# Key lengths applied to the token rows of the scores, and group normalisation in token layout, in a hybrid RWKV-7 and convolution decoder step

## The chip, the cores and the metric

The kernel runs on one core of a Trainium2 chip. The core has five engines that work side by side, each in the order of its own instruction list: PE (TensorE, matrix products and transposes into PSUM), DVE (VectorE), ACT (ScalarE), POOL (GpSimd) and SP (SyncE, which here only issues transfers). They wait for each other by semaphores. The metric is the device time of one execution in microseconds (us), lower is better; the median of several executions is compared.

## The reference, cut to what matters

One layer works on 1024 prompt tokens and on 8 short sample sequences of 4 tokens. The input is normalised and projected once; half of the mixing width goes through an RWKV-7 recurrence of 8 heads of 64 channels, the other half through a gated causal convolution; both meet in one output projection. Two places of it matter here: the division of each key by its length, and the two group normalisations over 64 channels of a token.

```python
kk = _heads(kf * k_k)
kk = kk / jnp.maximum(jnp.sqrt(jnp.sum(jnp.square(kk), axis=-1, keepdims=True)), 1e-12)
...
Sk = jnp.einsum('bhvk,bhk->bhv', S, kk_t)
S = S * w_t - Sk[..., None] * (kk_t * a_t)[:, :, None, :] + v_t[..., None] * k_t[:, :, None, :]
y_t = jnp.einsum('bhvk,bhk->bhv', S, r_t)
...
mean = jnp.mean(xg, axis=-1, keepdims=True)
var = jnp.mean(jnp.square(xg - mean), axis=-1, keepdims=True)
y = ((xg - mean) * lax.rsqrt(var + eps)).reshape(xf.shape)
```

The state S sees each normalised key twice in one product (`Sk` and `kk_t * a_t`), so the two inverse lengths of a token always come as their product, one over the squared length.

## The kernel before

**Work.** Channels lie on the 128 partitions, tokens along the free dimension. The input projection is done in blocks of 128 output channels and 256 tokens (`project`, tiles `ps`); its operands are split into a high and a low part (`whi`, `wlo`, `ha`/`hb`), so that each block takes 24 products. Recurrence work comes in units of two 128-channel rows (four heads) by 128 tokens, 16 units and one for the samples. A unit goes through `keys_unit`/`keys_unit2` (decay and keys), `scores_unit` with `masked_scores` (`ap`, `AB`, `Q`), the solution of a triangular system (`blocks_units`, `solve_units`, `solved_units`, `inverse_unit`), `chain_unit` (the recurrence over 64-token chunks, `cb`, `Yp`) and `post_unit` (group normalisation and bonus). The convolution has 16 pieces of 128 channels by 256 tokens (`convolutions`, `cv`), each followed by `post_conv` (group normalisation and swish). `gating` multiplies with the gates, `mixes` reloads the mixed rows, `outputs` does the output projection (`po`), `results` finishes the rows. The sample rows have parts of their own (`chain_sample`, `post_sample`, `outputs_sample`).

**Norms.** All 50 norms (17 of keys, 17 after the recurrence, 16 of the convolution) go through `inverse_norms`: two products with the squares as stationary operand and two columns of ones give sums by token (`n2`, from `arena`), DVE adds the guard, POOL raises to the power -0.5 (`nR`), ACT and POOL split the result into two parts (`nS`), two products with the identity turn it back to channel layout, ACT copies it (`nT`), and one product with `heads4` spreads it over the 64 channels of a head (`bc`), from where DVE multiplies. `group_norm` first takes the mean away by a product with the matrix `bcen` (`yc`).

**Order.** The code is written as some forty strands (generators). A planner (`_Schedule`) runs them at build time: each operation has a modelled cost, each strand a rank, and the operation that can start first is issued next on its engine, a higher rank first. So the order on every engine, SP's transfers included, is fixed before the kernel runs, and it follows from the modelled costs. The strand `filler`, the input projection, has the lowest rank and fills PE where nothing else is ready. All instructions are issued from line 341, so groups are told apart by the tiles they write and read. In the profile's names `n` is the tile `n2`, `arena` is the ring of working tiles, and trailing digits of names are left out.

Of the kernel before, what the change touches and what calls it, by code (L numbers as in the profile page):

```python
# [8 lines left out]
F32 = mybir.dt.float32  # L9
# [395 lines left out]
def hymba_step(ctx, tc, xp, xs, cT, ssT, w_ada, badag, gpost, w_in, wup, par, cst, wkv, cvs, w_out, wdd,  # L405
# [31 lines left out]
    nR = const.tile([128, 19], F32, name="nR")  # L437
    half = nR[:, 18:19]
# [7 lines left out]
    heads4 = const.tile([68, 128], F32R, name="heads4")  # L446
# [8 lines left out]
    for i in range(3):  # L455
        for h in range(2):
            r, a = slice(32 * i, 32 * i + 4), C_ID + 32 * i + h
            V.tensor_tensor(heads4[r, 64 * h:64 * h + 64], cs[r, a:a + 1].to_broadcast([4, 64]),
                            cs[r, a + 2:a + 3].to_broadcast([4, 64]), ALU.add)
# [4 lines left out]
    sl = _Slots({"raw": 2, "ga": 2, "whi": WB, "wlo": WB, "qa": 4, "kb": 2, "unit": 2, "wd": 2, "sh": 2, "wa": 8, "ts": 1, "d2": 2, "dt": 1, "ti": 2}, sched)  # L464
# [502 lines left out]
    def gate(x, p, g, t):  # L967

        keys = [("z", ("c", p), g)] if x == "c" else [("z", p // 2, 2 * g), ("z", p // 2, 2 * g + 1)]
        n = UN + 32 * (x == "c" and g == NU - 1)  # L970
# [81 lines left out]
    def proj_conv(j):  # L1052
# [15 lines left out]
        def ev_c(g, ps, t):  # L1068
            for o, x in parts(t, ps, g):
                S.activation(o, x, AF.Tanh, scale=0.5)  # L1070
                V.scalar_tensor_tensor(o, o, 1.0, x, ALU.add, ALU.mult)
            gate("c", j, g, t)
# [28 lines left out]
    nT = cp1.tile([128, 288], F32R, name="nT")  # L1101
    nRv = nR[:, 0:18].rearrange("p (r i h) -> p r i h", r=3, h=2)
    nS = cp1.tile([128, 3, 3, 4], F32R, name="nS")
    norms = [(r, nRv[:, r], nS[:, r]) for r in range(3)]

    def inverse_norms(nn, n, how, guard):

        while not norms:
            yield BLOCK
        r, R, Rs = x = norms.pop(0)  # L1110
        rows = slice(32 * r, 32 * r + 4)
        whole, rest = divmod(n, 128)
        n2 = yield from bank([128, 512], "n2")
        parts = [(slice(0, whole), 128)] + [(slice(whole, whole + 1), rest)] * (rest > 0)
        for ii, w in parts:
            for i in range(ii.start, ii.stop):
                T.matmul(n2[0:w, 2 * i:2 * i + 2], nn[:, 128 * i:128 * i + w], cs[:, C_ONE:C_ONE + 128:64], start=True, stop=True)
        for ii, w in parts:
            m = ii.stop - ii.start
            nv = n2[0:w, 2 * ii.start:2 * ii.stop].rearrange("p (i h) -> p i h", h=2)  # L1120
            V.tensor_scalar(R[0:w, ii], nv, guard, None, how)
            G.tensor_tensor(R[0:w, ii], R[0:w, ii], half[0:w].unsqueeze(2).to_broadcast([w, m, 2]), ALU.pow)
            S.activation(Rs[0:w, ii, 0:2], R[0:w, ii], AF.Copy)
            G.tensor_tensor(Rs[0:w, ii, 2:4], R[0:w, ii], Rs[0:w, ii, 0:2].bitcast(F32), ALU.subtract)
        for ii, w in parts:
            for i in range(ii.start, ii.stop):
                T.matmul(n2[rows, 128 + 128 * i:128 + 128 * i + w], Rs[0:w, i, :].bitcast(F32), ident[0:w, 0:w],
                         start=True, stop=True)
        S.activation(nT[rows, 0:n], n2[rows, 128:128 + n], AF.Copy)
        drop(n2)  # L1130
        yield
        bc = yield from bank([128, 512], "bc")
        T.matmul(bc[:, 0:n], heads4[rows], nT[rows, 0:n], start=True, stop=True)
        sched.later(lambda: norms.append(x))
        return bc
# [31 lines left out]
    def keys_unit2(p, g):  # L1167
# [5 lines left out]
        bc = yield from inverse_norms(nn, n, ALU.max, 1e-24)  # L1173
# [6 lines left out]
        V.tensor_tensor(kk[:, :n], kr[:, :n], bc[:, :n], ALU.mult)  # L1180
        drop(bc)
# [5 lines left out]
        mark(("keys", p, g), (E, Ei, kk, bt))  # L1187
        yield

    def keys_sample(p, g):  # L1190
# [10 lines left out]
        S.activation(nn[:, :n], kr[:, :n], AF.Square)  # L1201
# [17 lines left out]
    def keys_sample2(p, g):  # L1219
# [5 lines left out]
        bc = yield from inverse_norms(nn, n, ALU.max, 1e-24)  # L1225
# [7 lines left out]
        V.tensor_tensor(kk[:, :n], kr[:, :n], bc[:, :n], ALU.mult)  # L1233
        drop(bc)
# [6 lines left out]
        mark(("keys", p, g), (E, Ei, kk, bt))  # L1241
# [10 lines left out]
    def masked_scores(Q, KB, mask):  # L1252
# [10 lines left out]
        yield  # L1263
        for h in range(2):
# [4 lines left out]
            V.tensor_tensor(AB[H[h]].rearrange("p c a s -> p c (a s)")[:, :, a:128], aps[h][H[h], :, a:128],  # L1269
                            cs[H[h], mask + a:mask + 128].unsqueeze(1).to_broadcast([64, NCH, 128 - a]), ALU.mult)  # L1270
        for h in range(2):
# [7 lines left out]
    def scores_unit(p, g):  # L1279
# [4 lines left out]
        E, Ei, kk, bt = done["keys", p, g]  # L1284
# [12 lines left out]
        ec = w2.tile([128, 4], F32, tag="ec", name="ec", bufs=4)  # L1297
        V.tensor_copy(ec, tok65(E)[:, :, 64])
        give(E, Ei, kk, bt)
        for i, cc in both(p):  # L1300
            V.scalar_tensor_tensor(km[:, cc], km[:, cc], hp[:, 33 + i:34 + i], R[:, cc], ALU.mult, ALU.mult)
        AB = yield from masked_scores(Q, KB, C_MP)
        for c in range(NCH):
            S.activation(KB[:, c], KB[:, c], AF.Copy, scale=ec[:, c:c + 1])
        mark(("scores", p, g), dict(Q=Q, AB=AB, KB=KB, ec=ec))
# [16 lines left out]
    def scores_sample(p, g):  # L1322
# [3 lines left out]
        E, Ei, kk, bt = done["keys", p, g]  # L1326
# [14 lines left out]
        es = w1.tile([128, 4 * NB], F32, tag="es", name="es")  # L1341
# [736 lines left out]
```

## Time and profile before

| | |
|---|---|
| median of 3 runs | 866.58 us (866.39 to 872.11) |
| the profiled execution, its own time | 874.14 us |
| its span, first to last instruction | 872.4 us |
| mean granted TensorE clock in it | 0.975 |

The profiled execution is 7.6 us slower than the median. In the lists of the trace a row "x4" is four records; a product of full 32-bit operands leaves two records, one of the split parts or a transpose leaves one. The duration of a record reaches over the next ones, because products are pipelined: what a group costs PE is better read as the distance from its start to the start of the next group.

### The profile page before, as it was taken

To read this page: it belongs to the slowest core of one execution; us is meant where nothing else is said; L and a number is where in the kernel's file an instruction comes from. 1 tells how busy PE (TensorE), PEld (TensorE's weight loads), DVE (VectorE), ACT (ScalarE), POOL (GpSimd) and SP (SyncE) were. 2 spreads that over 40 slices of the span, in tenths; PEclk is the share of its full clock that TensorE was granted. 3 is DMA by queue.
4 is the path that set the end of the run, shared out by engine and by line. 5 is a ranking of instruction groups with operands and counts; after the bars stand their busy time and mean duration, and the time that the engine had idled before them with its cause. 6 is when DMAs were issued, how large, how long until landed. Compare 5 with 4: busy or idle time off the path is not lost.

```text
span 872.4 us, 23611 instructions
## 1 busy us (share of the span) xinstructions
PE 815.5 (93%) x9050; PEld 666.9 (76%) x9050; DVE 417.3 (48%) x1012; ACT 462.8 (53%) x1276; POOL 402.5 (46%) x759
## 2 busy tenths in 40 slices
PE   4868999999999999999999999999999999599995
PEld 2647888897889778888789878788987997475763
DVE  4556443562455554562662655574766363113122
ACT  4447577556676366672584567576655564211201
POOL 3237456463447216234325343644753765534332
PEclk9999899999999999999999999999999999698998
DMA  9987889788546753438735736435693676765432
GB/s 322 314 271 242 278 295 323 226 268 251 165 129 207 184 152 114 137 110 247 208 105 171 235 100 201 135 123 184 210 296 110 194 225 184 210 224 193 156 121 85
DMA packets 147729, 172.38 MB, mean 198 GB/s; under 512 B 23296, under 2 KB 105600, under 8 KB 147616
## 3 DMA queue, kind: packets, MB, share of 16 engines
q1 hardware_dynamic: 147328, 170.28, 63.0%
q8 instruction: 71, 1.16, 0.6%
q10 hardware_dynamic: 288, 0.59, 0.2%
q14 instruction: 42, 0.34, 0.1%
HBM read 112.68 MB, written 58.13 MB: 196 GB/s over the span
## 4 chain that ended last, share of the span: by engine, by line
PE 69%; DMA 14%; DVE 5%; ACT 4%; POOL 3%; issue 3%; SPq 1%; POOLq 0%; DVEq 0%; ACTq 0%
PE ps L341 30%; PE po L341 8%; PE cv L341 6%; PE n L341 4%; PE cb L341 4%; DMA wa<-w_ada 3%; PE ap L341 3%; PE Yp L341 2%; DMA xt<-xp 2%; PE yc L341 2%; PE p L341 2%; SPq L341 1%; PE bc L341 1%; DMA wd<-wdd 1%; ACT arena L341 1%
## 5 line engine op out<-in xcount | busy, mean ns | idle before, releaser
L341 PE MATMUL ps<-hb,whi 128*128 128x258 f32 (+3 forms) x928 | 199.0, 301 | 0.0
L341 PE MATMUL ps<-ha,whi 128*128 128x256 f32 (+2 forms) x864 | 180.9, 301 | 4.3 <-ACT ha L341 3.2
L341 PEld LDWEIGHTS ps<-hb,whi 128*128 128x128 f32 x928 | 149.6, 189 | 6.3 <-issue 2.7
L341 PEld LDWEIGHTS ps<-ha,whi 128*128 128x128 f32 x864 | 138.5, 191 | 14.8 <-issue 4.0
L341 PE MATMUL ps<-hb,wlo 128*128 128x258 f32 (+3 forms) x464 | 140.1, 302 | 0.0
L341 PE MATMUL ps<-ha,wlo 128*128 128x256 f32 (+2 forms) x432 | 130.9, 303 | 2.4 <-POOL wlo L341 2.4
L341 POOL TENSOR_TENSOR wlo<-raw,whi 128x512 fp32r<-128x512 f32 x58 | 78.4, 1352 | 66.1 <-ACT whi L341 50.2
L341 POOL TENSOR_TENSOR nR<-nR 128x4 f32<-128x4 f32 (+2 forms) x56 | 55.8, 998 | 77.5 <-DVE nR L341 77.2
L341 PEld LDWEIGHTS ps<-hb,wlo 128*128 128x128 f32 x464 | 87.6, 189 | 3.4 <-issue 1.2
L341 PEld LDWEIGHTS ps<-ha,wlo 128*128 128x128 f32 x432 | 82.4, 191 | 7.6 <-POOL wlo L341 3.0
L341 PE MATMUL cv<-SH,wd 128*32 128x256 f32 x1024 | 61.7, 389 | 4.0 <-DMA kept<-wlo 2.2
L341 ACT ACTIVATE arena<-ps,hp 128x256 f32<-128x256 f32 (+3 forms) x72 | 32.2, 455 | 51.7 <-PE ps L341 45.5
L341 ACT ACTIVATE X<-AB,cs 32x64 f32<-32x64 f32 x136 | 54.7, 403 | 2.1
L341 PEld LDWEIGHTS cv<-SH,wd 128*32 128x32 f32 x1024 | 35.1, 112 | 23.5 <-issue 2.7
L341 DVE SCALAR_TENSOR_TENSOR arena<-arena 128x256 f32<-128x256 f32 (+1 forms) x64 | 33.6, 527 | 34.3 <-DMA arena<-prj_a 13.1
L341 DVE TENSOR_TENSOR arena<-arena,bc 128x256 f32<-128x256 f32 (+2 forms) x50 | 20.6, 414 | 58.7 <-PE bc L341 56.2
L341 POOL TENSOR_TENSOR Ti<-Ti,tm 128x15 f32<-128x15 f32 (+4 forms) x135 | 41.1, 304 | 8.8
L341 ACT ACTIVATE whi<-raw 128x512 fp32r<-128x512 f32 x58 | 36.3, 626 | 15.6 <-DMA raw<-w_in 11.2
L341 POOL TENSOR_TENSOR tm<-D,Ti 128x15 f32<-128x15 f32 (+4 forms) x135 | 39.5, 293 | 10.2 <-DVE D L341 1.2
L341 ACT ACTIVATE arena<-arena 128x256 f32<-128x256 f32 (+3 forms) x100 | 41.1, 415 | 2.8 <-DVE ec L341 0.6
L341 DVE SCALAR_TENSOR_TENSOR arena<-ps,pr,arena 128x256 f32<-128x256 f32 (+4 forms) x40 | 17.5, 441 | 50.4 <-ACT arena L341 50.0
L341 POOL TENSOR_TENSOR arena<-arena,mx 128x256 f32<-128x256 f32 (+2 forms) x32 | 25.1, 785 | 35.3 <-ACT mx L341 31.8
(204 smaller groups left out, 1652.4 us busy)
## 6 DMA issues: line engine op xcount, KB each, us to landing
whi<-kept SPq DMA_DIRECT2D x52, 256.0 KB, 3.0
wlo<-kept SPq DMA_DIRECT2D x52, 256.0 KB, 3.8
raw<-w_in SPq DMA_DIRECT2D x50, 256.0 KB, 3.8
kept<-whi SPq DMA_DIRECT2D x44, 256.0 KB, 3.4
kept<-wlo SPq DMA_DIRECT2D x44, 256.0 KB, 3.2
wa<-w_ada SPq DMA_DIRECT2D x32, 256.0 KB, 5.4
SH<-gld SPq DMA_DIRECT2D x48, 142.0 KB, 4.0
xt<-xp SPq DMA_DIRECT2D x8, 512.0 KB, 5.4
```

The costliest lines, as they stand in the source:

```text
L341: emit = lambda: f(*a, **k)
```

## The change

Four things change.

1. `inverse_norms` is gone, with `nR`, `nS`, `nT` and `heads4`. For the keys, `square_sums` takes its place: eight products of a 64x64 block of squares with one column of ones, whose result lies with tokens on the partitions; DVE applies the guard (`n2s`).
2. The keys stay undivided (the product of `kr` with `bc` is left out). `scores_unit` takes the reciprocal of the squared lengths (`inv`, in the tile `er`), and `masked_scores` multiplies the token rows of the score block with it; this was a copy on ACT and is now a product on DVE. In `chain_unit` the two copies that negate the solved rows now multiply with `inv` (two ACT instructions and one DVE instruction where there were one and one), and the sign moves to the copy `Wt`.
3. `group_norm` transposes the tile to token layout (`tp`), takes the sum, the difference and the squares there (two reductions and two more operations on DVE, one square on ACT), raises and multiplies on POOL, and transposes back (`yc`). It returns the PSUM tile, and the caller's next operation reads it.
4. The 32 sample tokens of the convolution, which were appended to the last piece of each of four channel rows (288 columns), get a strand of their own, `post_conv_sample`, for all four rows; `gating` then always works on 256 columns.

```diff
+    def square_sums(nn):
+        n2 = yield from bank([128, NCH], "n2")
+        for u in range(NCH):
+            for h in range(2):
+                T.matmul(n2[H[h], u:u + 1], nn[H[h], 64 * u:64 * u + 64], cs[H[h], C_ONE + 64 * h:C_ONE + 64 * h + 1],
+                         start=True, stop=True)
...
+        V.tensor_scalar(t, n2, 1e-24, None, ALU.max)
...
-        bc = yield from inverse_norms(nn, n, ALU.max, 1e-24)
+        n2 = yield from square_sums(nn)
...
-        V.tensor_tensor(kk[:, :n], kr[:, :n], bc[:, :n], ALU.mult)
-        drop(bc)
...
+        V.reciprocal(inv, n2)
...
             if a:
-                S.activation(AB[H[h], :, 0, :], aps[h][H[h], :, 0:64], AF.Copy)
+                V.tensor_tensor(AB[H[h], :, 0, :], aps[h][H[h], :, 0:64], iv(h), ALU.mult)
...
-            S.activation(Wt, cb[:, 0], AF.Copy)
+            S.activation(Wt, cb[:, 0], AF.Copy, scale=-1.0)
...
-            S.activation(mv[H[0], :, c, 0, :], cb[H[0], 1], AF.Copy, scale=-1.0)
-            V.tensor_scalar(mv[H[1], :, c, 1, :], cb[H[1], 1], -1.0, None, ALU.mult)
+            for i, u in slots:
+                S.activation(MV[H[0], u, 0, :], cb[H[0], 1, i], AF.Copy, scale=inv[H[0], i, c:c + 1])
+            V.tensor_tensor(mv[H[1], :, c, 1, :], cb[H[1], 1], inv[H[1], :, c].unsqueeze(2).to_broadcast([64, 2, 64]), ALU.mult)
...
     def group_norm(src, n, guard):
-        yc = yield from bank([128, 512], "yc")
-        T.matmul(yc[:, :n], bcen, src, start=True, stop=True)
...
-        bc = yield from inverse_norms(q, n, ALU.add, guard)
-        V.tensor_tensor(q[:, :n], src, bc[:, :n], ALU.mult)
...
+        tp = yield from bank([128, 2, 128], "tp")
+        for i, w in tiles:
+            T.transpose(tp[0:w, i, :], src[:, 128 * i:128 * i + w], ident)
...
+            V.tensor_reduce(a, by_group(tp, ii, w), mybir.AxisListType.X, ALU.add)
+            V.tensor_scalar(a, a, 1.0 / 64, None, ALU.mult)
+            V.tensor_tensor(by_group(qv, ii, w), by_group(tp, ii, w), spread(a), ALU.subtract)
+            S.activation(sq[0:w, ii], qv[0:w, ii], AF.Square, scale=0.125)
+            V.tensor_reduce(b, by_group(sq, ii, w), mybir.AxisListType.X, ALU.add)
+            G.tensor_scalar(b, b, 1.0, guard, ALU.mult, ALU.add)
+            G.tensor_tensor(b, b, half[0:w].unsqueeze(2).to_broadcast([w, m, 2]), ALU.pow)
+            G.tensor_tensor(by_group(qv, ii, w), by_group(qv, ii, w), spread(b), ALU.mult)
...
+        for i, w in tiles:
+            T.transpose(yc[:, 128 * i:128 * i + w], qv[0:w, i, :], ident[0:w, 0:w])
...
+    def post_conv_sample():
+        yield from wait(*(("acc", j) for j in range(4)), *(("out", "c" + str(j), NU - 1) for j in range(4)))
...
+        Z.dma_start(out=mixd[4:8, :, SEQ:NT].rearrange("k p t -> p k t"), in_=side(z))
```

The planner makes a new order out of this. A program that lists each engine's instructions gives these pieces; a row is an instruction or several alike in a row (x2), `out<-in`, partitions x elements.

PE in the second half of the input projection, before, where the norms of three tiles meet recurrence work:

```order
L341 MATMUL bc<-nT,heads_126 128x256
L341 MATMUL za<-tw,wu 128x128 x2
L341 MATMUL cb<-Wt,TT 64x64 x4
L341 MATMUL n_7458<-cs,arena 128x2 x2
L341 MATMUL vt<-cs,arena 128x128 x2
L341 MATMUL yc<-arena,cs 128x256
L341 MATMUL ps<-hb,whi 128x256
L341 MATMUL n_7481<-cs,arena 128x2
L341 MATMUL cb<-MV,KTt 64x64 x4
L341 MATMUL Yp<-AB,MV 64x64 x2
L341 MATMUL n_7481<-cs,arena 128x2
```

The same engine and about the same place now:

```order
L341 MATMUL cv<-SH,wd 32x256 x32
L341 MATMUL cb<-MV,KTt 64x64 x4
L341 MATMUL Yp<-AB,MV 64x64 x4
L341 MATMUL n_7471<-cs,arena 64x1 x8
L341 MATMUL yc<-cs,arena 128x128 x2
L341 MATMUL tp<-cs,arena 128x128
L341 MATMUL kt<-cs,KB 128x128 x4
L341 MATMUL tp<-cs,arena 128x128 x3
```

In the place of the products `n`, `bc` and the wide `yc` stand single-column products and transposes.

PE at the samples' group normalisation in the output projection, before:

```order
L341 MATMUL yc<-arena,cs 128x160
L341 MATMUL po<-ha,mh 128x512 x2
L341 MATMUL po<-ha,ml 128x512 x2
L341 MATMUL n_10932<-cs,arena 128x2
L341 MATMUL n_10932<-cs,arena 32x2
L341 MATMUL n_10932<-cs,nS 4x128
L341 MATMUL n_10932<-cs,nS 4x32
L341 MATMUL bc<-nT,heads_126 128x160
L341 MATMUL po<-ha,mh 128x512 x2
```

And now:

```order
L341 MATMUL Yp<-Q,MV 64x64 x8
L341 MATMUL tp<-cs,arena 128x128
L341 MATMUL po<-ha,mh 128x512 x2
L341 MATMUL po<-ha,ml 128x512 x2
L341 MATMUL po<-ha,mh 128x512 x4
L341 MATMUL po<-ha,ml 128x512 x2
L341 MATMUL po<-ha,mh 128x512 x4
L341 MATMUL po<-ha,ml 128x512 x2
L341 MATMUL yc<-cs,arena 128x128
```

Four output products stood between `yc` and the first `n`, and none between the two kinds of `n`; now sixteen stand between the transpose there and the one back.

POOL at the same place (`hb<-wo` splits the output weights, `ml` the mixed rows, `nR` is the power), before:

```order
L341 TENSOR_TENSOR hb<-wo,hb 128x512 x3
L341 TENSOR_TENSOR nR<-nR 128x2
L341 TENSOR_TENSOR nR<-nR 32x2
L341 TENSOR_TENSOR nS<-nR,nS 128x2
L341 TENSOR_TENSOR ml<-raw,mh 128x512
L341 TENSOR_TENSOR hb<-wo,hb 128x512 x2
L341 TENSOR_TENSOR nS<-nR,nS 32x2
```

And now, with the statistics in `st`:

```order
L341 TENSOR_TENSOR ml<-raw,mh 128x512
L341 TENSOR_SCALAR st_205<-st_205 128x2
L341 TENSOR_TENSOR st_205<-st_205,half 128x2
L341 TENSOR_TENSOR hb<-wo,hb 128x512 x3
L341 TENSOR_TENSOR arena<-arena,st_205 128x128
```

The last POOL step of the norm stood behind two weight splits, and stands behind three.

More of the change, by code (lines that the diff above doesn't have):

```diff
@@ L1099, in tok65 @@
         return t[:, 0:260].rearrange("p (c s) -> p c s", s=65)
[L1101 to L1127, printed above, removed]
@@ L1128, in inverse_norms @@
+    norms = [cp1.tile([128, 2, 2, 2], F32, name=f"st{r}") for r in range(4)]
+    def square_sums(nn):
[3 more added lines that the diff above has]
+                T.matmul(n2[H[h], u:u + 1], nn[H[h], 64 * u:64 * u + 64], cs[H[h], C_ONE + 64 * h:C_ONE + 64 * h + 1],
                          start=True, stop=True)
-        S.activation(nT[rows, 0:n], n2[rows, 128:128 + n], AF.Copy)
+        yield from sl.need("n2")
+        t = w2.tile([128, NCH], F32, tag="n2", name="n2s", bufs=4)
+        V.tensor_scalar(t, n2, 1e-24, None, ALU.max)
@@ L1130, in inverse_norms @@
         drop(n2)
[L1131 to L1135, printed above, removed]
+        return t
     def keys_unit(p, g):
@@ L1186, in keys_unit2 @@
         give(nn)
-        mark(("keys", p, g), (E, Ei, kk, bt))
+        mark(("keys", p, g), (E, Ei, kk, bt, n2))
         yield
@@ L1345, in scores_sample @@
         V.tensor_tensor(pairwise(km), pairwise(km), per_pair(-33, 40), ALU.mult)
-        AB = yield from masked_scores(Q, KB, C_MS)
+        AB = yield from masked_scores(Q, KB, C_MS, inv)
         for a in range(2):
@@ L1664, in group_norm @@
     def group_norm(src, n, guard):
[L1666 to L1677 removed]
+        while not norms:
+            yield BLOCK
+        st = norms.pop(0)
+        whole, rest = divmod(n, 128)
+        parts = [(slice(0, whole), 128)] * (whole > 0) + [(slice(whole, whole + 1), rest)] * (rest > 0)
+        tiles = [(i, w) for ii, w in parts for i in range(ii.start, ii.stop)]
+        tp = yield from bank([128, 2, 128], "tp")
+        for i, w in tiles:
+            T.transpose(tp[0:w, i, :], src[:, 128 * i:128 * i + w], ident)
+        q = yield from take("nt", "q")
+        by_group = lambda t, ii, w: t[0:w, ii].rearrange("p i (h v) -> p i h v", h=2)
+        qv = q[:, 0:256].rearrange("p (i c) -> p i c", i=2)
+        sq = src[:, 0:256].rearrange("p (i c) -> p i c", i=2)
+        for ii, w in parts:
+            m = ii.stop - ii.start
+            spread = lambda a: a.unsqueeze(3).to_broadcast([w, m, 2, 64])
+            a, b = st[0:w, ii, :, 0], st[0:w, ii, :, 1]
+            V.tensor_reduce(a, by_group(tp, ii, w), mybir.AxisListType.X, ALU.add)
[6 more added lines that the diff above has]
+            G.tensor_tensor(by_group(qv, ii, w), by_group(qv, ii, w), spread(b), ALU.mult)
+        drop(tp)
+        yield
+        yc = yield from bank([128, 256], "yc")
+        for i, w in tiles:
+            T.transpose(yc[:, 128 * i:128 * i + w], qv[0:w, i, :], ident[0:w, 0:w])
+        sched.later(lambda: norms.append(st))
+        return q, yc
     def post_unit(p, g):
@@ L1842, in sample_block, with swish @@
         yield
+    def swish(z, q, yc, gains):
+        for cc, a, b in gains:
+            S.activation(z[:, cc], yc[:, cc], AF.Identity, scale=a, bias=b)
+        n = gains[-1][0].stop
+        drop(yc)
+        S.activation(q[:, 0:n], z[:, 0:n], AF.Tanh)
+        V.scalar_tensor_tensor(z[:, 0:n], q[:, 0:n], 1.0, z[:, 0:n], ALU.add, ALU.mult)
     def post_conv(first, step):
@@ L1859, in post_conv @@
             yield
+    def post_conv_sample():
+        yield from wait(*(("acc", j) for j in range(4)), *(("out", "c" + str(j), NU - 1) for j in range(4)))
+        z = yield from take("nt", "z")
+        side = lambda t: t[:, 0:128].rearrange("p (k t) -> p k t", k=4)
+        Z.dma_start(out=side(z), in_=accd.rearrange("k p t -> p k t"))
+        t = yield from take("gt", "gate")
+        for j in range(4):
+            Z.dma_start(out=t[:, 32 * j:32 * j + 32], in_=prj["c" + str(j)][:, SEQ:NT])
+        q, yc = yield from group_norm(z, 128, 1e-5)
+        swish(z, q, yc, [(slice(32 * j, 32 * j + 32), hp[:, 45 + j:46 + j], hp[:, 49 + j:50 + j]) for j in range(4)])
+        V.scalar_tensor_tensor(z[:, 0:128], z[:, 0:128], 0.5, t[:, 0:128], ALU.mult, ALU.mult)
+        Z.dma_start(out=mixd[4:8, :, SEQ:NT].rearrange("k p t -> p k t"), in_=side(z))
+        give(z, q, t)
+        mark(("mix", "cs"))
+        yield
     oq = []
@@ L1919, in outputs_sample @@
     def outputs_sample():
-        yield from wait("gates", ("y", 0, NE - 1), ("y", 1, NE - 1), ("mix", SMP), *(("mix", ("c", k), NU - 1) for k in range(4)))
+        yield from wait("gates", ("y", 0, NE - 1), ("y", 1, NE - 1), ("mix", SMP), ("mix", "cs"))
         m = yield from take("nt", "m")
```

94 lines of the change are left out of this document (45 added, 49 removed).

## The prediction

> **What bounds the kernel now.** I read the page first: the busy shares and the chain of work that ended last.
>
> ```profile
> span 872.4 us, 23611 instructions
> ...
> PE 815.5 (93%) x9050; PEld 666.9 (76%) x9050; DVE 417.3 (48%) x1012; ACT 462.8 (53%) x1276; POOL 402.5 (46%) x759
> ...
> PE 69%; DMA 14%; DVE 5%; ACT 4%; POOL 3%; issue 3%; SPq 1%; POOLq 0%; DVEq 0%; ACTq 0%
> ```
>
> PE is busy for all but 57 us and makes up most of the chain; the other engines are about half used. Next I cut the span into stretches (busy time of each engine, granted clock, share of the DMA engines) and asked what PE waited for.
>
> ```profile
> 100.00:200.00 100.00, 98.52 (x1067) 82.61 (x1069) 52.77 (x121) 64.17 (x173) 53.92 (x102) 0.97 0.88 286
> 600.00:700.00 100.00, 97.37 (x1111) 84.36 (x1110) 57.04 (x147) 57.15 (x163) 55.23 (x117) 0.98 0.65 201
> ...
> PE ada L341 <- DMA wa<-w_ada: 14.5, 8, 9.0
> PE n L341 <- POOL nS L341: 8.9, 2, 5.4
> ...
> POOL nR L341 <- DVE nR L341: 77.2, 32, 7.4
> ```
>
> From 100 us on PE hardly stops. Its largest wait lies ahead of that, the next is one place in the tail, and POOL waits much longer for PE's results than PE for POOL's. So a change counts here by the PE time it takes away or adds, if the new order keeps PE fed. How many norms there are, and where:
>
> ```profile
> L341 PE MATMUL n<-cs,arena x208: 165/251/273, 94.1 to 746.6; 128*128 128x2 f32 x98, 128*32 128x2 f32 x6
> L341 PE MATMUL n<-cs,nS x208: 184/273/418, 98.7 to 756.3; 128*4 128x128 f32 x98, 32*4 32x32 f32 x6
> L341 PE MATMUL bc<-nT,heads x50: 336/380/498, 100.9 to 756.9; 4*128 4x256 f32 x44, 4*128 4x288 f32 x4, 4*128 4x160 f32 x2
> L341 PE MATMUL yc<-arena,cs x66: 298/379/510, 149.7 to 745.1; 128*128 128x256 f32 x56, 128*128 128x288 f32 x8, 128*128 128x160 f32 x2
> ```
>
> Fifty `bc` are fifty norms; 66 records of `yc` are 33 group normalisations, so 17 norms are of keys. All lie between 94 and 757 us, where PE is the bound.
>
> **PE's part of the sum.** Two pieces of PE's timeline hold nearly every operation that goes, and the nearest rows to those that come (start, length, group).
>
> ```profile
> 319.72 0.38 PE L341 MATMUL bc<-nT,heads 4*128 4x256 f32 x1
> 320.02 0.66 PE L341 MATMUL kt<-cs,KB 128*128 128x128 f32 x4
> 320.52 0.60 PE L341 MATMUL bo<-arena,cs 128*128 128x256 f32 x2
> 320.95 0.59 PE L341 MATMUL yc<-arena,cs 128*128 128x256 f32 x2
> 321.48 0.45 PE L341 MATMUL cb<-Wt,TT 64*64 64x64 f32 x8
> 321.86 0.61 PE L341 MATMUL n<-cs,arena 128*128 128x2 f32 x4
> 322.32 0.41 PE L341 MATMUL vt<-cs,arena 128*128 128x128 f32 x2
> 322.49 0.38 PE L341 MATMUL ps<-hb,whi 128*128 128x296 f32 x1
> ...
> 733.79 2.04 PE L341 MATMUL sp<-Q,M 64*64 64x16 f32 x64
> 735.76 0.60 PE L341 MATMUL n<-cs,nS 128*4 128x128 f32 x4
> 736.29 0.51 PE L341 MATMUL po<-ha,mh 128*128 128x512 f32 x1
> ```
>
> From start to next start: `n` from `arena` 0.46, `n` from `nS` 0.53, `bc` 0.30, together 1.29 us for a norm; fifty are 64.5 us. `yc` took 0.53 here, and `bo`, of the same form, 0.43; I take 0.43, for 33 that is 14.2 us. Removed: 78.7 us. The ends are 64.5 + 33 x 0.24 = 72.4 (0.24 is half of the mean of `bo` and `yc`, one of the two records) and 64.5 + 17.5 = 82.
>
> Added for the keys: 17 times eight products, 16 records with 64x64 weights. The row nearest in columns is `sp`: 64 records in 1.97 us, so 16 in 0.49; the row nearest in place is `cb`: 8 in 0.38, so 0.76. Near the first, with a little for the changed shape, I take 0.55: 9.4 us (8.3 to 12.9).
>
> Added for the group normalisations: 67 transposes there and 67 back (two each, and one more of 32 tokens for the samples of each way). Four `kt` took 0.50, two `vt` 0.17; I take a pair at 0.25, the longer: 67 pairs, 16.8 us (11.4 to 16.8).
>
> Net: 78.7 - 9.4 - 16.8 = 52.5 us off PE, between 72.4 - 12.9 - 16.8 = 42.7 and 82 - 8.3 - 11.4 = 62.3.
>
> On transposes the Trainium skill speaks against the change: "TensorE: Matmul & The Clock Gate", Part 4, gives about 275 ns for one of 128x128 in a kernel's context and says that they do not count as activity for the clock. By that 134 would be an estimated 36.9 us and the net gain 32.4 us. The `kt` and `vt` rows, 0.125 and 0.085 us each, are for back-to-back ones in this kernel and disagree, and the granted clock was 1.00 from 150 to 200 us, with `kt` and `vt` in it (the rows of the stretches below), so the sum goes by them.
>
> **The other engines.** Durations of the removed operations and of the nearest ones to the new (busy time, mean ns of one, idle time before; the last row, of PE, is for a rival below):
>
> ```profile
> L341 POOL TENSOR_TENSOR nR<-nR 128x4 f32<-128x4 f32 x48 | 50.1, 1044 | 77.5 <-DVE nR L341 77.2
> L341 POOL TENSOR_TENSOR TT<-T,cs 128x256 f32<-128x256 f32 x17 | 11.5, 678 | 30.2 <-DVE T L341 30.2
> L341 DVE TENSOR_TENSOR arena<-arena,bc 128x256 f32<-128x256 f32 x44 | 18.2, 416 | 51.2 <-PE bc L341 50.8
> L341 DVE TENSOR_REDUCE accs<-arena 128x8 f32<-128x248 f32 x16 | 6.5, 406 | 6.0 <-POOL arena L341 5.9
> L341 ACT ACTIVATE AB<-ap 64x256 f32<-64x256 f32 x32 | 12.0, 376 | 9.7 <-PE ap L341 7.5 <-DVE Q L341 1.7
> L341 ACT ACTIVATE nT<-n 4x256 fp32r<-4x256 f32 x44 | 16.4, 373 | 22.9 <-PE n L341 22.1
> L341 PE MATMUL tp<-cs,xt 128*128 128x128 f32 x64 | 11.0, 317 | 2.6 <-DVE xt L341 2.6
> ```
>
> DVE: a group normalisation gains two reductions of about 0.41 (the new ones read 256 elements, the row 248) and loses nothing large, since the difference with 0.42 takes the place of the product with `bc`: 33 x 0.82 = 27 us. A unit of keys loses the product with `bc` and gains two products of 0.42 in `masked_scores`: 17 x 0.42 = 7 us. DVE goes from 417 to about 451 us, 55% of the new time. ACT loses `nT` fifty times and `AB` 32 times, 31 us. POOL loses 17 powers of 1.04 and gains 33 products of about 0.68: 5 us more. All of it lies beside PE: none of the three comes near PE's load, and what hides it is the projection (`ps`), which in the new order still stands between recurrence, transposes and convolution up to the first output products. If that cover were gone, a group normalisation would expose two reductions, a difference, a square, a power and a product in a row, 3.0 us by these rows with the square left aside, against a longer row of PE, DVE, POOL and ACT steps before. `chain_unit` gets a second ACT step in a row in each of its 32 steps; behind it wait only that unit's next products. The extra transfers (four loads and four stores of 32 columns for the samples' gate, fewer for `accd`) are six more on SP's queue by the lists of both programs. I count all this as nothing.
>
> **The tail.** The one long wait is in the samples' normalisation:
>
> ```profile
> 746.20 0.53 PE L341 MATMUL n<-cs,arena 128*128 128x2 f32 x4
> 752.15 0.59 PE L341 MATMUL n<-cs,nS 128*4 128x128 f32 x2 [5.42 <-POOL nS L341]
> 756.23 0.27 PE L341 MATMUL n<-cs,nS 32*4 32x32 f32 x2 [3.49 <-POOL nS L341]
> ...
> 753.33 2.50 POOL L341 TENSOR_TENSOR hb<-wo,hb 128x512 fp32r<-128x512 f32 x2
> 755.77 0.41 POOL L341 TENSOR_TENSOR nS<-nR,nS 32x2 fp32r<-32x2 f32 x1
> ...
> 815.82 21.38 PE po L341 x91
> ```
>
> POOL's steps stand behind splits of output weights that arrive late. In the new order sixteen output products (16 x 21.38 / 91 = 3.8 us, by the last row, from the chain) come in between, but the last POOL step stands behind three splits instead of two. I leave this wait as it is; its 9 us are the most that could be gained here.
>
> **What is taken off.** The transfers keep their volume while the projection gets shorter. The stretches where they are densest, with the records of `n` in each and the DMA share:
>
> ```profile
> 100.00:150.00 50.00, 2.31 (x16) 1.66 (x16) 0.33 (x2) 0.92 (x3) 0.93 0.93 309
> 150.00:200.00 50.00, 4.51 (x32) 3.17 (x32) 0.64 (x4) 1.49 (x4) 1.00 0.83 262
> 600.00:650.00 50.00, 3.77 (x28) 2.54 (x28) 0.54 (x4) 1.42 (x4) 1.00 0.75 228
> 700.00:750.00 50.00, 3.30 (x24) 2.31 (x24) 0.59 (x5) 0.77 (x2) 1.00 0.67 199
> ```
>
> The first two hold 48 of 416 records, 12% of the gain, 6 us; I take half of it as lost, 3 us, and as much again for new short waits of PE at the transposes back, which join POOL's queue. So 52.5 - 6 = 46.5 us. Against the profiled execution's own 874.1 us that is 827.6; against the median, 7.6 us lower, 820 us.
>
> **Rivals.**
> - *The gain holds* (70%): 820 us, from 803 (the upper net, nothing lost) to 838.
> - *Transfers hold it back* (12%): all four stretches of the last rows keep their length, 100 of 416 records or 24%, 13 us, and PE's waits for loads grow by as much again. Then 26 of the 52.5 us are lost: 866.6 - 52.5 + 26 = 840 us. For it speaks the share of 0.93, against it that PE there is still 98.5% busy.
> - *Transposes are dear* (6%): each advances PE by the whole mean length of such a record where the input is transposed, 0.317 us (row `tp` above), instead of 0.125: 134 x 0.317 = 42.5 us instead of 16.8, so 820 + 26 = 846 us. Against it: `kt` and `vt`, which stand in the same stretch of the program as the new ones. The Trainium skill's rule above ("TensorE: Matmul & The Clock Gate", Part 4) would come out near this, at an estimated 840.
> - *Waits take the place of the work* (7%): PE stops at each transpose back. The break-even is 52.5 / 33 = 1.6 us of waiting per normalisation, at which the time stays within 1% of 866.6. Against it: the same kind of join in the kernel before, fifty times, cost 8.9 us in all.
> - *Slower* (5%): POOL's queue becomes late as a whole, with its new last step (0.68 us) behind splits of 1.3 us. It decides from 1.85 us per normalisation (61 us); at half of the 5.42 us of the tail's wait, 2.7 us, the time is 866.6 - 52.5 + 89 = 903 us. For it speaks that such a wait exists; against it POOL's idle 77 us ahead of `nR`.
>
> That the operations stay is no rival: the lists of the new program hold none of the removed products.
>
> **How the numbers follow.** About 1% is what a measurement of this kernel can tell from no change. The first three cases are faster by more than that: 0.88; the fourth is the same, 0.07; the fifth slower, 0.05. The range from 802 to 844 takes in the first case and the second, 82%, and leaves out the other three.
>
> **What would show it.** In the new profile PE's busy time should be some 50 us lower, 94 to 97% of the part from 100 us to the first `po`; the first `po` should start some 45 us earlier; `tp` and `yc` pairs should advance by 0.25 us and the eight `n` by 0.55. DVE should show about 450 us, ACT about 430, POOL about 405. Wrong would be: PE waits for POOL's or DVE's normalisation steps of more than 10 us outside the tail, a lower granted clock between 100 and 700 us, or waits for `whi`, `wd` and `SH` loads that grow to tens of microseconds.

## The result and the profile after

| | kernel before | changed kernel |
|---|---|---|
| median, same chip | 869.35 us (866.39 to 878.21, 4 runs) | 833.25 us (829.40 to 835.91, 4 runs) |
| ratio of the two | | 0.9565, 95% interval 0.9481 to 0.9649 |
| the profiled execution, its own time | 874.14 us | 832.94 us |

The changed kernel is faster by 4.4%, some 36 us by the medians and 41.2 us between the two profiled spans (872.4 and 831.2 us). The profiled execution of before is 4.8 us above its median, that of the changed kernel at its median. The page of the changed kernel, its busy times and its chain of work:

```profile
span 831.2 us, 23357 instructions
...
PE 758.8 (91%) x8924; PEld 634.7 (76%) x8924; DVE 454.2 (55%) x1111; ACT 423.9 (51%) x1143; POOL 401.6 (48%) x753
...
PE 57%; DMA 20%; ACT 6%; DVE 6%; SPq 4%; issue 3%; POOL 2%; POOLq 0%; DVEq 0%; ACTq 0%
```

PE does 56.7 us less, DVE 37 more, ACT 39 less, POOL the same. PE's share of the chain fell from 69% to 57%: PE is still the bound, but it is fed less closely. The same is seen when the span is cut at the first output product (stretch, its length, PE's busy time and records, granted clock, share of the DMA engines, GB/s). First the kernel before:

```profile
100.00:723.00 623.00, 614.42 (x7696) 0.99 0.63 191
723.00:872.40 149.40, 126.12 (x721) 0.91 0.52 166
```

And the changed kernel:

```profile
100.00:690.40 590.40, 567.69 (x7695) 0.99 0.67 203
690.40:831.20 140.80, 116.59 (x586) 0.92 0.53 172
```

From 100 us to the first output product PE's busy time fell by 46.7 us, the stretch only by 32.6: PE's idle time there grew from 8.6 to 22.7 us. The tail lost 9.5 us of PE time and 8.6 us of length. What ended PE's waits between 100 us and the first output product, longest sums first (us in all, times, longest); the kernel before, and in the second fence the changed kernel:

```profile
PE cv L341 <- DMA kept<-wlo: 2.2, 1, 2.2
PE cv L341 <- DMA wd<-wdd: 1.7, 2, 1.1
PE yc L341 <- ACT arena L341: 1.0, 1, 1.0
```

```profile
PE cb L341 <- ACT MV L341: 3.0, 4, 0.8
PE cv L341 <- DMA wd<-wdd: 2.8, 2, 1.5
PE cv L341 <- DMA SH<-gld: 2.5, 3, 1.1
PE sp L341 <- DMA M<-wkv: 1.6, 1, 1.6
PE ps L341 <- POOL wlo L341: 1.5, 3, 0.6
PE kt L341 <- ACT KB L341: 1.4, 1, 1.4
PE cb L341 <- issue: 1.3, 1, 1.3
PE cv L341 <- DMA whi<-kept: 1.3, 1, 1.3
```

No single wait explains the 14 us: there are many of 1 to 3 us, more than a third of their sum for loads. The longest sum is new: products of the recurrence (`cb`) that wait for ACT's scaled rows `MV`, a step that the change made longer. PE's waits for the normalisation steps of DVE and POOL do not appear, outside one place in the tail. The new operations in the table by line and form (busy time, mean ns of one, idle time of the engine before them):

```profile
L341 PE MATMUL tp<-cs,arena 128*128 128x128 f32 x66 | 13.9, 284 | 1.0 <-ACT arena L341 0.8 <-ACT TT L341 0.2
L341 PE MATMUL n<-cs,arena 64*64 64x1 f32 x272 | 11.1, 194 | 0.1
L341 DVE TENSOR_REDUCE st<-tp 128x4 f32<-128x256 f32 x32 | 13.4, 421 | 12.2 <-PE tp L341 12.0
L341 POOL TENSOR_TENSOR arena<-arena,st 128x256 f32<-128x256 f32 x32 | 20.3, 636 | 1.7
L341 ACT ACTIVATE MV<-cb,er 64x64 f32<-64x64 f32 x64 | 18.6, 308 | 27.9 <-PE cb L341 13.0 <-DVE MV L341 10.4 <-POOL tm L341 4.0
L341 DVE TENSOR_TENSOR MV<-cb,er 64x128 f32<-64x128 f32 x32 | 9.4, 295 | 30.8 <-ACT MV L341 24.0 <-POOL Ti L341 3.3 <-POOL arena L341 1.2
```

The last two rows are the recurrence's step. Each names the other as what ended its waits (10.4 and 24.0 us), and in the trace ACT's and DVE's parts of a step never overlap; in 21 of the 32 steps the DVE instruction stands between the two of ACT. From the start of the first instruction of a step to the end of the last, the median step takes 1.05 us. In the kernel before, with these two rows (shortest, median and longest in ns; 32 of the 33 are of the chain), it takes 0.67 us:

```profile
L341 ACT ACTIVATE MV<-cb x33: 258/270/377, 163.6 to 741.9; 64x128 f32<-64x128 f32 x32, 64x256 f32<-64x256 f32 x1
L341 DVE TENSOR_SCALAR MV<-cb x33: 294/294/429, 164.0 to 742.4; 64x128 f32<-64x128 f32 x32, 64x256 f32<-64x256 f32 x1
```

Over 32 steps, at 0.38 us each, the chain is some 12 us longer, of which PE waits for as much as it has no other work for.

The tail keeps its long wait. PE and POOL there (start, length, group, idle time before it):

```profile
704.06 0.62 PE L341 MATMUL po<-ha,ml 128*128 128x512 f32 x2
704.52 1.09 PE L341 MATMUL po<-ha,mh 128*128 128x512 f32 x4
705.45 0.63 PE L341 MATMUL po<-ha,ml 128*128 128x512 f32 x2
714.38 0.47 PE L341 MATMUL yc<-cs,arena 128*128 128x128 f32 x1 [8.29 <-POOL arena L341]
...
717.27 1.22 PE L341 MATMUL po<-ha,mh 128*128 128x512 f32 x2 [1.14 <-ACT arena L341]
718.29 0.63 PE L341 MATMUL po<-ha,ml 128*128 128x512 f32 x1
718.71 1.91 PE L341 MATMUL po<-ha,mh 128*128 128x512 f32 x4
```

```profile
709.57 0.71 POOL L341 TENSOR_TENSOR st<-st,half 128x2 f32<-128x2 f32 x1
710.25 3.72 POOL L341 TENSOR_TENSOR hb<-wo,hb 128x512 fp32r<-128x512 f32 x3
713.91 0.41 POOL L341 TENSOR_TENSOR arena<-arena,st 128x128 f32<-128x128 f32 x1
```

The samples' last normalisation step (713.91) stands behind three weight splits of 3.72 us, which PE waits for. But the chain that ended last does not run through POOL here. It runs through the load of the mixed rows (start, length, what):

```profile
712.27 3.13 DMA raw<-mixd
...
716.05 1.18 ACT arena L341 x4
717.22 0.04 issue
717.27 0.80 PE po L341
```

ACT splits these rows first (from 715.51) and reads `yc` only then (716.05), and PE's second wait, of 1.14 us, ends with that. By these rows a shorter queue on POOL alone would move three records of output products ahead, and not the rest.

After the second wait three records of output products take 1.44 us (717.27 to 718.71), 0.48 each, where two took 0.46 together ahead of the long wait (704.06 to 704.52); the granted clock says why (stretches of 5 us of the changed kernel):

```profile
700.00:705.00 5.00, 5.00 (x37) 1.00 0.87 261
705.00:710.00 5.00, 1.08 (x5) 0.94 0.59 194
710.00:715.00 5.00, 0.62 (x2) 0.50 0.54 158
715.00:720.00 5.00, 3.86 (x10) 0.50 0.50 138
720.00:725.00 5.00, 5.00 (x17) 0.69 0.71 203
```

The clock is at half some 3 us after PE's last product (which ended at 706.1; 0.94 is full clock up to about 709.4), and the 0.69 puts its return at about 723, some 9 us after PE's work began again, with the second wait in between. PE worked between 7 and 8 us at half rate, so by this estimate the wait of 8.3 us costs three to four more. The Trainium skill ("TensorE: Matmul & The Clock Gate", Part 1) states such a gate, half rate after an idle window of about 3.4 us and full rate after a busy window of that length; the rows agree on the first and show a longer way back, which holds the second wait. The kernel before pays about the same at its own wait (clock 0.50 from 750 to 760 us, 0.66 from 760 to 765), so this is no difference between the two.

### The profile page after: what moved, and what is told of

Same layout as the page of the kernel before. It is cut to its first block, busy times and chain, and to the rows that moved or that the text cites. A ratio compares the mean times of both kernels' runs of the same rounds, so it can differ in the third digit from the quotient of the medians.

```text
span 831.2 us, 23357 instructions
## 1 busy us (share of the span) xinstructions
PE 758.8 (91%) x8924; PEld 634.7 (76%) x8924; DVE 454.2 (55%) x1111; ACT 423.9 (51%) x1143; POOL 401.6 (48%) x753
## 4 chain that ended last, share of the span: by engine, by line
PE 57%; DMA 20%; ACT 6%; DVE 6%; SPq 4%; issue 3%; POOL 2%; POOLq 0%; DVEq 0%; ACTq 0%
PE ps L341 25%; PE po L341 10%; PE cv L341 5%; SPq L341 4%; PE cb L341 4%; ACT arena L341 3%; DMA SH<-gld 3%; PE Yp L341 2%; DMA gld<-arena 2%; PE ap L341 2%; DMA kept<-whi 2%; DMA arena<-prj_a 2%; DVE arena L341 2%; DMA xt<-xp 1%; DMA arena<-zd 1%
## 5 line engine op out<-in xcount | busy, mean ns | idle before, releaser
L341 PE MATMUL ps<-ha,whi 128*128 128x256 f32 (+2 forms) x864 | 178.6, 300 | 3.8 <-ACT ha L341 2.9
L341 PE MATMUL cv<-SH,wd 128*32 128x256 f32 x1024 | 58.6, 380 | 7.9 <-DMA wd<-wdd 2.8
L341 ACT ACTIVATE arena<-arena 128x256 f32<-128x256 f32 (+5 forms) x103 | 41.7, 409 | 16.2 <-DVE arena L341 11.4
L341 PE MATMUL po<-ha,mh 128*128 128x512 f32 x128 | 40.2, 433 | 2.5 <-DVE M L341 1.4
L341 ACT ACTIVATE mh<-raw 128x512 fp32r<-128x512 f32 x16 | 10.1, 631 | 57.5 <-DMA raw<-mixd 47.0
L341 DVE TENSOR_TENSOR Q<-arena 64x256 f32<-64x256 f32 (+1 forms) x68 | 36.6, 540 | 0.6
```

The lines of the kernel that those rows point to most:

```text
L341: emit = lambda: f(*a, **k)
```

## The experiments

The first theory was that the PE work taken off is the whole gain, and that what is missing was lost to waits which the change itself made: the longer step of the recurrence and the samples' wait in the tail. The rival was that the planner's new order decides: any edit changes the modelled costs, the planner places hundreds of instructions otherwise, and the time moves with that. Runs e1 to e4 ran on one chip (kernel before 872.97 us, 7 runs), e5 to e8 on a second (869.24 us, 11 runs), e9 to e12 on a third (869.60 us, 23 runs). Each ratio is to the kernel before on the same chip, so runs of different chips are better compared by their ratios.

**e1, the keys' part alone.** From the kernel before: `square_sums`, `inv`, the scores and `chain_unit` of the change; `group_norm` as it was.

```diff
-        bc = yield from inverse_norms(nn, n, ALU.max, 1e-24)
+        n2 = yield from square_sums(nn)
```

> The kernel before with the key part of the change alone (squared lengths applied to token rows, no transposes). Theory 1 (the gain is PE work, the loss is many small waits spread over the program): PE busy falls by 11 to 13 us against before (17 norms at 1.29 less 0.55), PE's idle time between 100 and 700 us rises by 3 to 5 us, the time falls by 8 to 10 us, to about 858. Rival (the second ACT step in the recurrence carries most of the 15 us of new waits): PE idle rises by 8 us or more here, waits of cb for ACT MV of 3 us and more, and the time falls by 4 us or less.

Measured: 859.42 us, ratio 0.9858 (0.9808 to 0.9908). PE's busy time is 800.7 us, 14.8 less than before. From 100 to 700 us PE is idle for 12.8 us instead of 8.6, as theory 1 had it, and its waits of `cb` for ACT's `MV` sum to 1.0 us. The time fell by more than theory 1's 8 to 10 us, and the gain stands in the tail: the first output product starts at 724.2 us instead of 723.0, and the tail is 132.9 us long instead of 149.4.

**e2, the group normalisation alone.** From the changed kernel: the keys divided and normed as before, and the recurrence's step as before.

```diff
-        n2 = yield from square_sums(nn)
+        bc = yield from inverse_norms(nn, n, ALU.max, 1e-24)
```

> The kernel before with the group normalisation part alone (transposes; keys still divided through the old norms). Theory 1: PE busy falls by 40 to 46 us, PE idle rises by 8 to 12 us, the time falls by some 32 us, to about 836. Rival (the waits belong to the key part): PE idle stays within 4 us of before's 38 and the time falls by 40 us or more, to under 829.

Measured: 844.33 us, ratio 0.9677 (0.9644 to 0.9711). PE's busy time is 779.6 us, 35.9 less than before. The two parts save 13.6 and 28.6 us; together that is 42 us, where the whole change saves 36 to 37 (e5). The keys' part gave about what the prediction's terms make of it (17 x 1.29 - 9.4 = 12.5 us), though where it gave it owes something to the order; the normalisation's part gave less (33 x 1.29 + 14.2 - 16.8 = 40 us). Ahead of the first output product, which starts at 664.9 us here, PE is idle for 7.1 us, less than before. So the 14 us of new idle time there are not the sum of the two parts: the keys' part alone shows 4 of them, the normalisation alone none. In the tail of e2 PE waits 5.2 us for finished output rows of DVE and 4.2 us for POOL at a transpose back.

**e3, both halves of the solved rows scaled on DVE.** The changed kernel without the two ACT instructions of the recurrence's step.

```diff
-            for i, u in slots:
-                S.activation(MV[H[0], u, 0, :], cb[H[0], 1, i], AF.Copy, scale=inv[H[0], i, c:c + 1])
-            V.tensor_tensor(mv[H[1], :, c, 1, :], cb[H[1], 1], inv[H[1], :, c].unsqueeze(2).to_broadcast([64, 2, 64]), ALU.mult)
+            for h in range(2):
+                V.tensor_tensor(mv[H[h], :, c, h, :], cb[H[h], 1], inv[H[h], :, c].unsqueeze(2).to_broadcast([64, 2, 64]), ALU.mult)
```

> The changed kernel, but both halves of the solved rows are multiplied on DVE, so the recurrence has one DVE step more and no ACT step there. If the second ACT step costs what the waits of cb for ACT MV show (3.0 us in four places), those waits go and the time falls by about 3 us against the changed kernel, to 830. If PE's small waits only move to the next late operand: the waits for ACT MV go, waits for DVE come, the time stays within 1% of 833.

Measured: 822.48 us, ratio 0.9415 (0.9357 to 0.9472), 1.5% below the changed kernel's and more than either expectation. The step is now two DVE instructions, 0.61 us, and PE's idle time between 100 us and the first output product is halved:

```profile
L341 DVE TENSOR_TENSOR MV<-cb,er 64x128 f32<-64x128 f32 x64 | 18.5, 289 | 27.6 <-PE cb L341 22.0 <-POOL arena L341 1.9 <-POOL st L341 1.8
...
100.00:657.60 557.60, 545.89 (x7399) 1.00 0.68 206
```

11.7 us idle instead of 22.7. But some 40% of the rows of PE's list stand in another order than in the changed kernel, and the first output product starts 33 us earlier with more other work behind it. So this alone does not tell the step from the order.

**e4, the samples' last normalisation product on DVE.**

```diff
-            G.tensor_tensor(by_group(qv, ii, w), by_group(qv, ii, w), spread(b), ALU.mult)
+            (V if n < UN else G).tensor_tensor(by_group(qv, ii, w), by_group(qv, ii, w), spread(b), ALU.mult)
```

> The changed kernel, but the last product of the samples' normalisation runs on DVE, which is idle there, not behind three weight splits on POOL. If POOL's queue sets the tail, the 8.3 us wait at the transpose back falls to about 4 us and the end comes 3 to 4 us earlier (829). If the mixed rows, which arrive by transfers at 715 us, set it, the wait at the transpose falls as much, but PE then waits as long at the next output products, and the time stays at 833.

Measured: 827.05 us, ratio 0.9471 (0.9419 to 0.9523); the intervals of the changed kernel, 0.9481 to 0.9649 and 0.9523 to 0.9618 (e5), overlap or touch this one. In the traces the order of PE is the changed kernel's up to 749 us, but for three records. The wait is shorter and the tail with it, 135.1 instead of 140.8 us:

```profile
PE yc L341 <- DVE arena L341: 5.0, 1, 5.0
...
688.50:823.60 135.10, 115.51 (x586) 0.93 0.55 174
```

What remains of the wait is POOL's power, which stands behind other work of POOL, and the product on DVE, which takes 1.34 us there while POOL splits weights, against 0.41 us on POOL in the changed kernel. Two more things differ at this very place: the mixed rows land at 711.9 us instead of 715.4, and ACT splits them behind its reading of `yc` instead of ahead of it. So e4 does not tell POOL's queue from the mixed rows.

**e5, the changed kernel again**, as the base of the next three.

> The changed kernel unaltered, on the chip of the next three runs, as their base. Both theories: a ratio to the kernel before of 0.956 within 0.008, about 834 us where the kernel before takes 872.

Measured: 833.63 us (830.55 to 835.15, 6 runs), ratio 0.9571 (0.9523 to 0.9618).

**e6, e3 and e4 together.**

> The two edits of e3 (both halves of the solved rows scaled on DVE) and e4 (the samples' last normalisation product on DVE) together. Theory (the second ACT step of the recurrence costs some 11 us, the wait in the tail up to 7): the gains lie in different stretches, projection and tail, and add up: 11 us from the first, 3 to 6 from the second, so 815 to 820 us, a ratio of 0.935 to 0.940. Rival (each edit only led the planner to a luckier order): no better than the better of the two, 822 us or more, ratio 0.942 or more.

Measured: 823.29 us, ratio 0.9438 (0.9389 to 0.9486): no better than e3, as the rival had it. In this order the long wait is another one, as it already was in e3: PE waits for POOL's product of a 256-column tile, which the edit leaves on POOL.

```profile
PE yc L341 <- POOL arena L341: 5.0, 2, 4.5
```

**e7, the kernel before with its ACT step split in two**, the planner free to make a new order.

```diff
-            S.activation(mv[H[0], :, c, 0, :], cb[H[0], 1], AF.Copy, scale=-1.0)
+            for i, u in slots:
+                S.activation(MV[H[0], u, 0, :], cb[H[0], 1, i], AF.Copy, scale=-1.0)
```

> The kernel before with nothing changed but the negation of the solved rows' first half, done in two ACT instructions of 64 columns instead of one of 128. Theory (the longer chain step is what cost the changed kernel part of its gain): each of 32 chain steps gets about 0.3 us longer, and the time rises by 4 to 11 us, less than the full sum where the longer PE work of this kernel covers more of it: ratio 1.005 to 1.013. Rival (the step is hidden as the prediction had it): ratio within 0.997 to 1.003.

Measured: 855.41 us, ratio 0.9841 (0.9789 to 0.9892). Neither expectation: with 32 instructions more the kernel is 1.6% faster. Its profiled execution, at 864.36 us the longest of its six, shows where most of that is, in the tail; ahead of it the first output product starts 6 us later than before:

```profile
729.20:862.30 133.10, 117.36 (x656) 0.97 0.58 181
```

The tail is 133.1 us instead of 149.4, with 15.7 us instead of 23.3 not busy and the clock at 0.97 instead of 0.91. The samples' wait of 8.9 us is not in its list of waits; the new order happened to put it elsewhere. The split step itself is hardly longer in this trace, 0.71 us by the median instead of 0.67, since ACT's two instructions overlap. So the order is worth more here than the step that was meant to be measured.

**e8, the changed kernel with one number of the planner changed.** The instructions stay, only the modelled latency of a load differs.

```diff
-            end = self.dma + 2.2
+            end = self.dma + 2.4
```

> The changed kernel with nothing changed but the planner's modelled latency of a load, 2.4 instead of 2.2 us: the instructions stay, their order changes in many places. Theory: the order as such is worth little, the time stays within 4 us of e5. Rival (differences of about 10 us come from the order that the planner happens to find, and then e3 and e4 show nothing of their own edits): the time moves by 7 us or more, either way.

Measured: 842.19 us, ratio 0.9678 (0.9625 to 0.9732), 8.6 us more than e5. The rival again. The first output product starts 20 us earlier than in the changed kernel, but the tail is 27.5 us longer: PE has more work there, waits for a load of the samples' state, and its clock falls to 0.88:

```profile
PE sp L341 <- DMA M<-wkv: 11.2, 3, 5.5
...
670.30:838.60 168.30, 130.05 (x865) 0.88 0.49 152
```

After this, orders were held: the planner plans as for the unaltered kernel, and only what an instruction of the plan emits is altered. The lists of e9 to e11 are those of their base on every engine but for the altered instruction.

**e9, the changed kernel with one ACT instruction in the recurrence's step, order held.**

```diff
+            first, second = sched.cur.queue[-2:]
+            first.emit = lambda: None
+            second.emit = lambda o=mv[H[0], :, c, 0, :], s=cb[H[0], 1]: nc.scalar.activation(o, s, AF.Copy, scale=-0.001)
```

> The changed kernel with its order held on every engine; only the two ACT instructions for the first half of the solved rows are one instruction again, at the place of the second of them. The scale of that half is a constant, so its rows are not divided by the squared lengths: the work and the waits are timed, not the values. Theory A (the second ACT step lengthens the recurrence's chain and PE waits for it): PE's waits for ACT's MV and the idle time of the projection fall, 5 to 11 us less than e5, 823 to 829 us, ratio 0.944 to 0.951. Theory B (the order that the planner finds decides, the step itself is covered): within 3 us of e5, 831 to 837 us, ratio 0.954 to 0.961.

Measured: 829.74 us, ratio 0.9545 (0.9506 to 0.9584), 3.9 us below e5 by the medians and 2.3 by the ratios, between the two expectations by the first and inside theory B's by the second; the intervals overlap. The step is 0.60 us here instead of 1.05, so a chain that is 14 us shorter gave back 2 to 4 us, if any. The profile shows the wait itself shrink: PE's waits for `MV` ahead of `cb`, 3.0 us in the changed kernel, are

```profile
PE cb L341 <- ACT MV L1550: 0.8, 2, 0.4
```

**e10, the kernel before with the split step, order held.**

```diff
+            pair = [(MV[H[0], u, 0, :], cb[H[0], 1, i]) for i, u in slots]
+            sched.cur.queue[-1].emit = lambda pair=pair: [nc.scalar.activation(o, s, AF.Copy, scale=-1.0) for o, s in pair]
```

> The kernel before with its order held on every engine; only the one ACT instruction for the first half of the solved rows is two, as in e7, where the planner was free to make a new order. Theory A: 4 to 11 us slower than before, ratio 1.005 to 1.013. Theory B: the step is covered, ratio 0.997 to 1.004, and the 1.6% that e7 was faster came from its order alone.

Measured: 872.32 us (12 runs), ratio 1.0049 (1.0013 to 1.0085): slower by about half a percent, 1 to 7 us. The same edit that was 1.6% faster with a free order costs a little with a held one; the whole gain of e7 was its order. As in e7 the split makes a step only 0.04 us longer, some 1 us over the 32, against 12 in the change; so this run does not price the longer step of the change. The row of the split step:

```profile
L1564 ACT ACTIVATE MV<-cb 64x64 f32<-64x64 f32 x64 | 10.4, 211 | 16.6 <-PE cb L341 9.7 <-DVE MV L341 4.1 <-POOL nR L341 1.9
```

**e11, each transpose of the group normalisation issued twice, order held.**

```diff
+            again = sched.cur.queue[-1]
+            again.emit = lambda f=again.emit: (f(), f())
```

> The changed kernel with its order held on every engine and each of the 134 transposes of the group normalisation issued twice. If a transpose advances PE by 0.085 to 0.125 us, as the prediction's sum has it, 11 to 17 us more than e5, all of it on PE's path: 845 to 851 us, ratio 0.970 to 0.977. If it is 0.275 to 0.317 us, as the rival has it, 37 to 42 us more: 870 us or more, ratio 0.999 or more. If PE has slack there, less than 6 us more.

Measured: 841.32 us, ratio 0.9667 (0.9628 to 0.9707), 7.7 us more than e5 for 134 transposes (8.3 by the ratios): some 0.06 us each, between the first expectation and the last. PE's busy time rose by 16.8 us, 0.125 each:

```profile
PE 776.0 (92%) x9058; PEld 649.8 (77%) x9058; DVE 455.1 (54%) x1111; ACT 423.6 (50%) x1143; POOL 401.0 (48%) x753
```

The profiled span grew by 12.2 us against e5's 829.1, 0.09 each. Part of the added work filled gaps in which PE had waited: its idle time is 65.3 us, 69.9 in e5. A price of 0.275 us and more is excluded.

**e12, the kernel before with the planner's number changed as in e8.**

> The kernel before with nothing changed but the planner's modelled latency of a load, 2.4 instead of 2.2 us, the same as e8 for the changed kernel. If the order as such is worth about 10 us either way (theory B, by e7 and e8), the time differs from before by 5 us or more; if the kernel before stands at a typical order, it lies between 855 and 880 us. Theory A: within 4 us of before, ratio 0.995 to 1.005.

Measured: 867.08 us (12 runs), ratio 0.9973 (0.9942 to 1.0003): within the measurement of the kernel before, as theory A had it, so not every new order moves the time. Its tail lost the samples' wait, too (131.5 us, clock 0.96), but its first output product starts 10 us later than before.

```profile
732.80:864.30 131.50, 117.78 (x655) 0.96 0.58 183
```

## Why the prediction was right, and where its sizes were off

The likeliest case came true: faster, inside the range, because PE's work went and PE stayed the bound. By the prediction's steps, in the profiled executions:

| step | prediction | measured |
|---|---|---|
| PE's work | 52.5 us less (42.7 to 62.3) | 56.7 less |
| waits in the dense stretches, 100 to 200 us | 3 more | 4.1 more |
| other new waits, up to the first output product | 3 more | 10.0 more |
| waits before 100 us and in the tail | no change | 1.4 more |
| sum | 46.5 less | 41.2 less |

The second row is the difference of PE's busy time in 100 to 200 us, 98.5 before and 94.4 in these two rows of the changed kernel:

```profile
100.00:150.00 50.00, 46.49 (x549) 0.97 0.96 309
150.00:200.00 50.00, 47.94 (x584) 1.00 0.88 280
```

*PE's terms.* By the distances from start to next start, added over all records, the removed products were 71.8 us (forecast 78.7), the eight `n` of a unit of keys 0.56 us (0.55), a pair of transposes 0.18 us (0.25). The net of these is 50.1 us, close to the forecast 52.5 because two misses, of 6.9 and 4.7 us, partly cancel. The busy time fell by 6.6 us more than that; what makes up the rest was not taken apart. The rival of dear transposes is refuted by e11. The Trainium skill's figure ("TensorE: Matmul & The Clock Gate", Part 4, about 275 ns) is near the duration of a record, 284 ns in the row `tp` above, but it is not what a transpose costs PE here. Nor did the transposes cost clock, which is 0.99 as before between 100 us and the first output product.

*The term that was mis-sized* is what is taken off for waits: 6 us, where 15.5 came. Two sentences of the prediction stand behind it. The one on the recurrence, "behind it wait only that unit's next products", is true but not worth nothing: the chain became some 12 us longer, and where the projection does not cover it, PE waits, 3.0 us for `MV` by the list above. With the order held, e9 points to 2 to 4 us for the longer step without separating it from nothing; e10, whose step is hardly longer, cannot price it. The prediction had also not counted that the split step's scale is read from a tile: an ACT instruction of this shape took 308 ns with it and 211 ns with a constant (e10). The Trainium skill ("ScalarE: Activation LUTs", What ACT_TABLE_LOAD costs) gives 93 ns for such an operand, and the rows agree with 97. The other sentence, on 3 us of short waits at the transposes back, named the wrong place: those waits hardly exist, and in their stead stand many small ones, for loads of the convolution and for ACT. Shown is that they are there, and that neither part of the change alone brings as many (e1 and e2). That they come from less PE work to cover the same transfers is not shown, and no run took the loads apart.

*What it said the new profile would show.* DVE at about 450, ACT 430 and POOL 405 us came as 454, 424 and 402, and PE's share from 100 us to the first output product, 94 to 97%, as 567.69 / 590.40 = 96.2%. The first output product came 32.6 us earlier instead of 45, since the new waits stand ahead of it; the tail gave the other 8.6 us. None of the three signs of a wrong prediction appeared.

*The tail.* "I leave this wait as it is" held: 8.9 us before, 8.3 after, again at POOL's weight splits. That it is a place to gain at e4 suggests, at about 1%, but the mixed rows came earlier there, too. What the prediction did not see is that the chain past the wait runs through those rows, and that the wait also halves the clock behind it, in both kernels.

*What is no step of the prediction* is the order. Orders of nearly the same instructions gave 855.4 (e7), 867.1 (e12) and about 869.5 us for the old norms, and 822.5 (e3), 823.3 (e6), 827.1 (e4), 833.6 (e5) and 842.2 us (e8) for the new. The change's 36 us stand clear of that, the slowest of the new order being 13 us under the fastest of the old; but no forecast by terms of a few microseconds can be nearer than some 10 us here. So e3's 11 us cannot be put down to the ACT step alone: e9 supports at most a third of it.

The predicted 820 us was 13.3 under the median: 5.3 from the terms above, and the rest almost all from carrying over the 7.6 us by which the profiled execution of before lay above the median then known. Later medians of the kernel before were 3 to 6 us higher, and the changed kernel's profiled execution lies at its median. The ends of the prediction's first case do not follow exactly from its terms, either: 866.6 - 62.3 is 804, not 803, and with the lowest net and 6 us lost the slow end is 830, where 838 is stated without its working. The measured 833.25 us lies within the stated end, but beyond 830.

The kernel of e3 beats both: the change with both halves of the step on DVE, 822.48 us.

## What to carry to other kernels

Work taken off the bounding engine comes back as time in large part, not in full: here 56.7 us of PE's busy time were 36 us by the medians and 41 between the profiled spans, and 16.8 us added in a held order cost 8 to 12. Count every dependent chain that becomes longer as well, since there is less work left to cover it. Where a planner makes the order, an edit is measured together with a new order; hold the order and alter only what is emitted before a few microseconds are put down to an instruction. Before such a run is read, look in its trace whether the edit made the step as much longer as was meant. And a wait of TensorE of several microseconds should be looked at with the granted clock behind it, not by its length alone.

## What the runs showed that was not expected

- After a wait of 8.3 us the clock was 0.50 until about 723 us, and three records of output products took 0.48 us each, where two ahead of the wait took 0.46 together.
- Two ACT instructions of 64 columns with a constant scale, one behind the other (e10), made a step only 0.04 us longer than one of 128 columns, 0.71 instead of 0.67 us.
- 134 more transposes, in a held order, cost 7.7 us by the medians and 12.2 between profiled spans, though PE's busy time rose by 16.8: an engine that is 91% busy still takes a part of such work into its gaps.
- A change of one planner constant by 0.2 us moved the changed kernel by 1.0% and the kernel before by nothing that could be told, and an added instruction in 32 places made the kernel before 1.6% faster.
